# A hybrid layer: second norm's squares with the out-projection, its gain on up's weights, three groups' first products ahead, w_down's sums paced

## The chip, the cores and the metric

One core of a Trainium2 chip. The metric is device time in microseconds of one launch, as the median of several runs. The core has five engines that run their own instruction queues in order: PE (matmuls), DVE and ACT (elementwise work), POOL, and SP, which issues nearly all transfers here. "fp32r" is the type in which the kernel gives its float32 operands to PE.

## The reference

One layer on 1040 positions (16 meta tokens and 1024 tokens), width 1024:

```python
hn = rms_norm(h, norm1_gain)
proj = einsum('bld,de->ble', hn, w_in)
mixed = concat([diff_attention(q, k, v, ...), conformer_conv(u, ...)])
h = h + einsum('ble,ed->bld', mixed, w_out)
hn = rms_norm(h, norm2_gain)
a = relu(einsum('bld,df->blf', hn, w_up))      # 1024 -> 4096
h = h + einsum('blf,fd->bld', a * a, w_down)   # 4096 -> 1024
return h[:, N_META:]
```

with rms_norm(x, g) = x * rsqrt(mean(x * x) + 1e-6) * g, all in float32.

## The kernel before

The 1024 tokens are eight tiles of 128. Every product is made of three matmuls (`three`, L331), since each operand is split into a rounded part (hi, a copy on ACT) and the rest (lo, a difference on DVE); `halves` (L813) makes such a pair. The up- and down-projections use a Strassen scheme: the matrices are cut in 2 x 2 blocks, so that seven products take the place of eight, at the price of sums of blocks on DVE.

The stages follow one another: first norm and input projection, convolution, attention in 32 units with the convolution's out-projection between them, the attention's out-projection (`attn_out`, L696: one half of 512 columns of one tile; it loads the convolution's part, adds the product, stores h2 to DRAM), second norm, up, down. Of the 16 halves of `attn_out` eight lie among the attention units, for tiles 7 to 4, and use one of the two PSUM banks of the tag "x"; the other eight are `late_out` (L988), for tiles 3 to 0, behind attention.

The second norm is `normed(t)` (L830): it loads a tile of h2 again from DRAM (tile 0 is kept on chip), squares it on ACT (L839), takes the inverse root in two POOL steps (L124, L125), multiplies by it and by the gain row `grow` on DVE (xn, L845), and transposes xn on PE into two PSUM banks. The gain row is made at the very start by eight small matmuls, two copies and two stores (L172 to L183). `norm_first` (tiles 7 to 4) makes the operands 11 and 21; `norm_second` (tiles 3 to 0) combines them with its own rows into t1 to t4 and 22 (L866).

Up works in 16 groups of 256 columns of w_up. `up_prep(g)` loads four cells of 128 x 512 (tag "wr", six buffers, 256 KB each), sums them and writes seven pairs (tag "wp", six buffers). A group's products are numbered: 1 and 2 need only the operands of `norm_first`, 6, 4, 7, 5 and 3 need those of `norm_second`. For NE = 2 groups `up_early` (L974) makes products 1 and 2 in the middle of the norms. Product 3 of a group (`up_last`, L953) is made in the next group, with the four sums that become down's operands; they go to DRAM (asp). `down_sums` (L941) loads 2 MB of w_down, forms four sums in place and stores them (wsp); it is called in every second group.

The order on each engine's queue is set by a scheduler at build time: it goes through the instructions by priority (program order, mostly), with a model of their times, and takes what it believes ready; a tile of a tag waits for a free buffer of this tag. On the chip each queue then runs in this fixed order.

## Time and profile before

| | |
|---|---|
| median of 3 runs | 1186.49 us (1185.21 to 1188.16) |
| the profiled execution | 1185.49 us, span 1183.7 us, mean granted clock 0.983 |
| PE busy | 1112.7 us, 94% of the span |
| DVE busy | 819.4 us, 69% |
| ACT busy | 561.8 us, 47% |
| POOL busy | 135.9 us, 11% |
| transfers | 189.67 MB, mean 160 GB/s |

The span runs from the first to the last instruction. A table of stretches gives each engine's busy time in a piece of the span; the granted clock is the share of TensorE's full speed, 1.00 for 2.4 GHz. In a time line the bracket behind a row tells how long the engine stood idle before it and what ended that.

### The profile page before, as it was taken

What the parts mean: (1) busy time and instruction counts of PE and PEld (TensorE: products, weight loads), DVE (VectorE), ACT (ScalarE), POOL (GpSimd) and SP (SyncE); (2) the same over time, 40 slices, a digit from 0 to 9 for tenths busy, and PEclk for the clock granted to TensorE, in tenths of its full rate; (3) what the DMA queues carried; (4) which work ended last, traced back from release to release, by engine and by line L of the source; (5) the groups of instructions that cost most, each with busy time, mean ns of one, the idle gap of its engine ahead of it and who ended that gap; (6) DMA issues with size and microseconds to landing.
All of it is one profiled execution on the core that took longest, in us unless ns stands there. A gap on an engine that the chain in (4) does not pass through costs nothing.

```text
span 1183.7 us, 15731 instructions
## 1 busy us (share of the span) xinstructions
PE 1112.7 (94%) x5712; PEld 935.9 (79%) x5712; DVE 819.4 (69%) x1366; ACT 561.8 (47%) x1230; POOL 135.9 (11%) x145
## 2 busy tenths in 40 slices
PE   3999999999999999785999999999989999999998
PEld 2899888777788888674778877788868888888887
DVE  5669989967788788679678868866647544445430
ACT  6522155607767677546345545555636332333320
POOL 3100274414002252111000000000000000000000
PEclk9999999999999999898899999999999999999999
DMA  7302011000123321572699999844369765556610
GB/s 279 108 1 73 1 37 37 5 24 27 37 71 107 105 93 53 177 231 92 229 322 324 325 340 310 293 149 135 127 233 402 267 241 215 208 199 227 215 56 36
DMA packets 103230, 189.67 MB, mean 160 GB/s; under 512 B 7904, under 2 KB 42976, under 8 KB 97520
## 3 DMA queue, kind: packets, MB, share of 16 engines
q1 hardware_dynamic: 103152, 188.66, 46.1%
q8 instruction: 45, 0.74, 0.3%
q14 instruction: 33, 0.27, 0.1%
HBM read 129.39 MB, written 59.24 MB: 159 GB/s over the span
## 4 chain that ended last, share of the span: by engine, by line
PE 65%; DVE 14%; DMA 9%; issue 5%; ACT 4%; POOL 2%; SPq 0%; DVEq 0%; POOLq 0%; ACTq 0%
PE py L335 5%; PE py L333 5%; PE py L334 5%; PE px L334 5%; PE px L335 5%; PE px L333 5%; DMA wr<-in_w_up 3%; PE pu L334 3%; PE pu L335 3%; PE pu L333 3%; PE pq L334 2%; PE pq L335 2%; PE pq L333 2%; DMA wdr<-in_w_down 2%; DVE wp L816 2%
## 5 line engine op out<-in xcount | busy, mean ns | idle before, releaser
L816 DVE TENSOR_TENSOR pair<-rv,pair 128x2048 fp32r<-128x2048 f32 x56 | 126.7, 2288 | 120.2 <-ACT pair L815 120.2
L815 ACT ACTIVATE pair<-rv 128x2048 fp32r<-128x2048 f32 x56 | 105.1, 1911 | 169.2 <-PE py L335 85.7
L333 PE MATMUL py<-pair 128*128 128x512 f32 x256 | 99.6, 389 | 0.0
L334 PE MATMUL py<-pair 128*128 128x512 f32 x256 | 99.6, 389 | 0.0
L335 PE MATMUL py<-pair 128*128 128x512 f32 x256 | 99.6, 389 | 0.0
L333 PE MATMUL px<-pair 128*128 128x512 f32 x192 | 74.7, 389 | 0.0
L334 PE MATMUL px<-pair 128*128 128x512 f32 x192 | 74.7, 389 | 0.0
L335 PE MATMUL px<-pair 128*128 128x512 f32 x192 | 74.7, 389 | 0.0
L333 PE MATMUL pu<-xT,w 128*128 128x260 f32 x256 | 73.1, 288 | 1.2 <-ACT xT L128 1.2
L334 PE MATMUL pu<-xT,w 128*128 128x260 f32 x256 | 73.6, 288 | 0.0
L335 PE MATMUL pu<-xT,w 128*128 128x260 f32 x256 | 73.2, 286 | 0.0
L935 ACT ACTIVATE a<-a 128x512 f32<-128x512 f32 x64 | 39.3, 629 | 61.5 <-DVE a L819 31.8
L333 PE MATMUL px<-hnt,wp 128*128 128x512 f32 x128 | 51.8, 404 | 13.1 <-ACT hnt L815 9.6
L124 POOL TENSOR_SCALAR ms<-ss 128x1 f32<-128x1 f32 (+3 forms) x34 | 37.3, 1097 | 203.5 <-ACT junk L391 137.6
L815 ACT ACTIVATE wp<-wr 128x512 fp32r<-128x512 f32 x64 | 39.7, 626 | 43.2 <-PE pw L335 22.5
L819 DVE TENSOR_TENSOR wdr<-wdr 128x1024 f32<-128x1024 f32 x32 | 39.0, 1220 | 29.0 <-DMA wdr<-in_w_down 14.8
L335 PEld LDWEIGHTS py<-pair 128*128 128x128 f32 x256 | 48.0, 188 | 10.0
L334 PEld LDWEIGHTS py<-pair 128*128 128x128 f32 x256 | 48.0, 188 | 10.0
L333 PEld LDWEIGHTS py<-pair 128*128 128x128 f32 x256 | 48.0, 188 | 9.9
L815 ACT ACTIVATE wp<-s 128x512 fp32r<-128x512 f32 x48 | 30.1, 628 | 52.1 <-PE px L335 30.7
L334 PE MATMUL px<-hnt,wp 128*128 128x512 f32 x128 | 51.4, 402 | 1.5 <-DVE hnt L816 1.5
L335 PE MATMUL px<-hnt,wp 128*128 128x512 f32 x128 | 51.4, 402 | 0.0
(296 smaller groups left out, 3204.3 us busy)
## 6 DMA issues: line engine op xcount, KB each, us to landing
rv<-as SPq DMA_DIRECT2D x28, 1024.0 KB, 6.2
wr<-in_w_up SPq DMA_DIRECT2D x68, 256.0 KB, 4.6
as<-a SPq DMA_DIRECT2D x64, 256.0 KB, 3.4
wdr<-in_w_down SPq DMA_DIRECT2D x8, 2048.0 KB, 9.7
ws<-wdr SPq DMA_DIRECT2D x32, 512.0 KB, 4.0
rv<-ws SPq DMA_DIRECT2D x16, 1024.0 KB, 4.8
as<-as SPq DMA_DIRECT2D x48, 256.0 KB, 3.6
rv<-in_w_down SPq DMA_DIRECT2D x12, 1024.0 KB, 6.0
```

Of the source, the lines that this page charges most:

```text
L124: RS.tensor_scalar(ms, ss, eps, None, ALU.add)
L333: T.matmul(ps, st[0], mv[0], start=first, stop=False, skip_group_check=more)
L334: T.matmul(ps, st[0], mv[1], start=False, stop=False, skip_group_check=more)
L335: T.matmul(ps, st[1], mv[0], start=False, stop=last, skip_group_check=more)
L815: S.activation(hi, src, AF.Copy)
L816: (eng or V).tensor_tensor(out=lo, in0=src, in1=hi.bitcast(F32), op=ALU.subtract)
L819: eng.tensor_tensor(out=out, in0=a, in1=b, op=ALU.subtract)
L935: S.activation(c, c, AF.Relu)
```

## The change

The squares of the second norm are taken by `attn_out` from its own sum, half by half, with the result of the squaring written over the product's PSUM bank; the inverse roots `rs2` follow there. All tiles of `late_out` stay on chip (four buffers of half a tile), and the first two halves are made ahead of the first norms. In `normed` xn is now one ACT copy with the scale `rs2`, without the gain; reloaded tiles use the buffers "wr". The gain is put on w_up's rows after their load, in place on ACT, four pieces a load (`wload`), so the gain row and its making go. "wr" has two buffers of 512 KB, "wp" has seven.

Products 1 and 2 are made ahead for three groups, after all norms in program order, both in one PSUM bank; their two results go to DRAM and come back when the group's turn comes. In the group loop `up_last` moves behind product 2, and product 5 ahead of 7. The eight `down_sums` are spread over groups 0 to 11, and each begins with a copy on DVE that reads a result of its group, ahead of its load.

```diff
--- before.py
+++ after.py
@@ -48,11 +48,12 @@
 QDI = 1
 WR = 2
 W1T = 5
-UT = 7
-WRB = 6
+UT = 8
+WRB = 2
 WSB = 3
-WPB = 6
-NE = 2
+WPB = 7
+NE = 3
+HKB = 4
 RVB = 4
 
 
@@ -167,20 +168,6 @@
         nc.sync.dma_start(xs[0][:, t, :], x[t * P:(t + 1) * P, :])
     gains = cp.tile([P, 2, 8], F32, tag="gains", name="gains")
     nc.sync.dma_start(gains, ngains)
-
-
-    growd = dr.tile([P, D], F32, tag="growd", name="growd")
-    ones = sp.tile([P, P], F32, tag="tmp", name="ones", bufs=4)
-    G.memset(ones, D ** 0.5)
-    for hf in range(2):
-        bank = tr_bank("gtr")
-        for q in range(4):
-            dg = sp.tile([P, P], F32, tag="tmp", name="dg", bufs=4)
-            V.tensor_scalar(dg, ident, gains[:, 1, 4 * hf + q:4 * hf + q + 1], None, ALU.mult)
-            T.matmul(bank[:, q, :], ones, dg, start=True, stop=True)
-        gr = sp.tile([P, 512], F32, tag="tmp", name="gr", bufs=4)
-        S.activation(gr, bank.rearrange("p a b -> p (a b)"), AF.Copy)
-        nc.sync.dma_start(growd[:, 512 * hf:512 * hf + 512], gr)
 
     xT = []
     for c in range(4):
@@ -692,18 +679,25 @@
 
     h2d = [dr.tile([P, D], F32, tag=f"h2d{t}", name=f"h2d{t}") for t in range(NT)]
     h2t = {}
+    ssq = cp.tile([P, NT, 2], F32, tag="ssq", name="ssq")
+    rs2 = cp.tile([P, NT], F32, tag="rs2", name="rs2")
 
     def attn_out(pool, t, nh, keep=None):
+
         if keep is None:
             hs = tmp([P, 512], F32, "hs")
         else:
-            if nh == 0:
-                h2t[t] = keep.tile([P, D], F32, tag="h2k", name="h2k", bufs=1)
-            hs = h2t[t][:, 512 * nh:512 * nh + 512]
+            hs = keep.tile([P, 512], F32, tag="h2k", name="h2k", bufs=HKB)
+            h2t.setdefault(t, []).append(hs)
         nc.sync.dma_start(hs, cvo[t, nh])
         ps = half_out(pool, ma, state[0, nh], t)
         V.tensor_tensor(out=hs, in0=hs, in1=ps, op=ALU.add)
         nc.sync.dma_start(h2d[t][:, 512 * nh:512 * nh + 512], hs)
+        S.activation(ps, hs, AF.Square, scale=D ** -0.5, accum_out=ssq[:, t, nh:nh + 1])
+        if nh:
+            ms = small([P, 8], "ms", 4)[:, :1]
+            G.tensor_scalar(ms, ssq[:, t, 0:1], ssq[:, t, 1:2], EPS, ALU.add, ALU.add)
+            G.tensor_tensor(out=rs2[:, t:t + 1], in0=ms, in1=mhalf[:, :1], op=ALU.pow)
 
     uqs, pend = [], []
     for t in range(NT):
@@ -822,8 +816,6 @@
         eng.tensor_tensor(out=out, in0=a, in1=b, op=ALU.add)
 
 
-    grow = up.tile([P, D], F32, tag="wp", name="grow", bufs=WPB)
-    nc.sync.dma_start(grow, growd)
     hn = {}
     hraw = slot([P, 2, 4, 512], F32, "hraw")
 
@@ -832,18 +824,13 @@
         if t in h2t:
             hv = h2t[t]
         else:
-            hv = up.tile([P, D], F32, tag="wp", name="h2t", bufs=WPB)
-            nc.sync.dma_start(hv, h2d[t])
-        ss = small([P, 1], "ss")
-        junk = sp.tile([P, D], BF16, tag="tmp", name="junk2", bufs=4)
-        S.activation(junk, hv, AF.Square, accum_out=ss)
-        rs = small([P, 1], "rs")
-        rsqrt_of(rs, ss, D * EPS)
+            h2 = up.tile([P, D], F32, tag="wr", name="h2t", bufs=WRB)
+            nc.sync.dma_start(h2, h2d[t])
+            hv = h2[:, :512], h2[:, 512:]
         banks = []
         for kf in range(2):
-            xn = tmp([P, 512], F32, "xn")
-            V.scalar_tensor_tensor(xn, hv[:, 512 * kf:512 * kf + 512], rs[:, 0:1],
-                                   grow[:, 512 * kf:512 * kf + 512], ALU.mult, ALU.mult)
+            xn = sp.tile([P, 512], F32, tag="raw", name="xn", bufs=4)
+            S.activation(xn, hv[kf], AF.Copy, scale=rs2[:, t:t + 1])
             bank = pcm.tile([P, 4, P], F32, tag="mm", name="htr")
             for q in range(4):
                 T.transpose(bank[:, q, :], xn[:, q * P:(q + 1) * P], ident)
@@ -869,25 +856,26 @@
                 operand(name)
         r11, r21 = [hraw[:, j, :, col(t):col(t) + P] for j in range(2)]
         b12, b22 = normed(t)
-        r12, t1, t2, t4 = [cell(n) for n in ("r12", "t1", "t2", "t4")]
-        S.activation(r12, b12, AF.Copy)
+        t1, t2, t3, t4 = [cell(n) for n in ("t1", "t2", "t3", "t4")]
         sub(V, t1, b12, r11)
         sub(V, t2, b22, t1)
         halves(*parts("t2", t), t2)
         sub(V, t4, t2, r21)
         halves(*parts("t4", t), t4)
-        sub(V, r12, b22, r12)
-        halves(*parts("t3", t), r12)
+        sub(V, t3, t2, r11)
+        halves(*parts("t3", t), t3)
         halves(*parts("t1", t), t1)
         halves(*parts("22", t), b22)
 
 
     wu = {}
 
-    def wcell(g, j, c):
-        r = cell("wr", "wr", WRB)
-        nc.sync.dma_start(r, w_up[512 * j:512 * j + 512, 256 * g + P * c:256 * g + P * c + P].rearrange(
-            "(k p) f -> p k f", p=P))
+    def wload(g, j, n):
+
+        r = up.tile([P, 4, n], F32, tag="wr", name="wr", bufs=WRB, padded_shape=[P, 4, 256])
+        nc.sync.dma_start(r, w_up[512 * j:512 * j + 512, 256 * g:256 * g + n].rearrange("(k p) f -> p k f", p=P))
+        for k in range(4):
+            S.activation(r[:, k, :], r[:, k, :], AF.Copy, scale=gains[:, 1, 4 * j + k:4 * j + k + 1])
         return r
 
     def wpair(g, n, v):
@@ -896,11 +884,12 @@
         halves(*wu[g, n], v)
 
     def prep_early(g):
-        wpair(g, 1, wcell(g, 0, 0))
-        wpair(g, 2, wcell(g, 1, 0))
+        wpair(g, 1, wload(g, 0, P))
+        wpair(g, 2, wload(g, 1, P))
 
     def up_prep(g):
-        l11, l12, l21, l22 = [wcell(g, j, c) for c in range(2) for j in range(2)]
+        l1, l2 = [wload(g, j, 256) for j in range(2)]
+        l11, l21, l12, l22 = l1[:, :, :P], l1[:, :, P:], l2[:, :, :P], l2[:, :, P:]
         if g >= NE:
             wpair(g, 1, l11)
             wpair(g, 2, l12)
@@ -909,9 +898,9 @@
         sub(V, s2, s1, l11)
         wpair(g, 6, s2)
         wpair(g, 4, l22)
+        wpair(g, 5, s1)
         sub(V, l21, l11, l21)
         wpair(g, 7, l21)
-        wpair(g, 5, s1)
         sub(V, s4, l12, s2)
         wpair(g, 3, s4)
 
@@ -938,9 +927,10 @@
     asp = {(n, b): dr.tile([P, 4, 512], F32, tag=f"as{n}{b}", name=f"as{n}{b}") for b in range(4) for n in range(1, 8)}
     wsp = {(n, b): dr.tile([P, 4, 512], F32, tag=f"ws{n}{b}", name=f"ws{n}{b}") for b in range(4) for n in range(4, 8)}
 
-    def down_sums(g):
+    def down_sums(g, after):
 
         r = slot([P, 2, 2, D], F32, "wdr")
+        V.tensor_copy(r[:, 0, 0, 0:1], after[:, 0:1])
         nc.sync.dma_start(r, w_down[256 * g:256 * g + 512, :].rearrange("(q j p) n -> p q j n", j=2, p=P))
         r11, r12, r21, r22 = [r[:, :, j, 512 * k:512 * k + 512] for j in range(2) for k in range(2)]
         sub(V, r11, r12, r11)
@@ -964,66 +954,68 @@
         sub(V, a21, a11, a21)
         sub(V, s4, a12, s2)
         for n, v in ((1, a11), (2, a12), (4, a22), (5, s1), (6, s2), (7, a21), (3, s4)):
-            nc.sync.dma_start(asp[n, g // 4][:, g % 4, :], v)
-
-    def erow(name):
-        return up.tile([P, 512], F32, tag="e", name=name, bufs=2 * NE)
-
-    early = {}
+            if n > 1 or g >= NE:
+                nc.sync.dma_start(asp[n, g // 4][:, g % 4, :], v)
+
+    es = [dr.tile([P, 512], F32, tag=f"es{g}", name=f"es{g}") for g in range(NE)]
 
     def up_early(g):
+
         px = bank("px")
         up_product(g, 1, px, True)
-        s1 = erow("s1")
+        s1 = row("s1")
         S.activation(s1, px, AF.Copy)
-        py = bank("py")
-        up_product(g, 2, py, True)
-        a11 = erow("a11")
-        add(V, a11, s1, py)
-        relu2(a11)
-        early[g] = s1, a11
+        nc.sync.dma_start(es[g], s1)
+        up_product(g, 2, px, False)
+        a11 = row("a11")
+        S.activation(a11, px, AF.Relu)
+        S.activation(a11, a11, AF.Square)
+        nc.sync.dma_start(asp[1, g // 4][:, g % 4, :], a11)
 
     late = [(7 - k // 2, k % 2) for k in range(len(AOUT), 16)]
 
     def late_out(n):
         for _ in range(n):
             tn = late.pop(0)
-            attn_out(pcm, *tn, keep=None if tn[0] else up)
-
+            attn_out(pcm, *tn, keep=up)
+
+    late_out(2)
     for t in (7, 6):
         norm_first(t)
     late_out(2)
     for t in (5, 4):
         norm_first(t)
+    for g in range(NE):
+        prep_early(g)
     late_out(2)
-    prep_early(0)
     norm_second(3)
-    late_out(2)
-    up_early(0)
-    prep_early(1)
     norm_second(2)
     late_out(2)
-    up_early(1)
+    up_prep(0)
     norm_second(1)
-    up_prep(0)
     norm_second(0)
-
+    for g in range(NE):
+        up_early(g)
+
+    sums_at = {(8 * k) // 5: 2 * k for k in range(8)}
     held = None
     for g in range(NG):
-        if g in early:
-            s1, a11 = early.pop(g)
+        if g < NE:
+            s1, a11 = row("s1"), row("a11")
+            nc.sync.dma_start(s1, es[g])
+            nc.sync.dma_start(a11, asp[1, g // 4][:, g % 4, :])
         else:
             px = bank("px")
             up_product(g, 1, px, True)
             s1 = snap(px)
-        if held:
-            up_last(held)
-        if g >= NE:
             py = bank("py")
             up_product(g, 2, py, True)
             a11 = row("a11")
             add(V, a11, s1, py)
             relu2(a11)
+        if held:
+            up_last(held)
+        if g >= NE:
             up_product(g, 6, px, False)
             s2 = snap(px)
         else:
@@ -1035,23 +1027,22 @@
             up_prep(g + 1)
         pz = bank("pz")
         up_product(g, 4, pz, True)
+        pw = bank("pw")
+        up_product(g, 5, pw, True)
         up_product(g, 7, px, False)
         if g >= NE:
             s3 = snap(px)
         else:
             s3 = s1
             add(V, s3, s1, px)
-        a12 = row("a12")
+        a12, a22 = row("a12"), row("a22")
+        add(V, a22, s3, pw)
         sub(V, a12, s3, pz)
         relu2(a12)
-        pw = bank("pw")
-        up_product(g, 5, pw, True)
-        a22 = row("a22")
-        add(V, a22, s3, pw)
         relu2(a22)
         held = g, s2, pw, (a11, a12, a22)
-        if g % 2 == 0:
-            down_sums(g)
+        if g in sums_at:
+            down_sums(sums_at[g], s2)
     up_last(held)
     up_pool.__exit__(None, None, None)
     ps_c.__exit__(None, None, None)
```

## Rows read from the trace of the kernel before

**Rows 1.** Table of stretches: time, busy us per engine, clock, DMA share, GB/s.
```profile
431.00:491.60 60.60, 59.96 (x412) 52.03 (x410) 50.94 (x152) 43.65 (x143) 15.65 (x20) 1.00 0.19 62
491.60:571.00 79.40, 52.46 (x229) 42.29 (x229) 59.77 (x99) 41.26 (x79) 10.12 (x18) 0.81 0.60 193
571.00:760.00 189.00, 185.67 (x805) 151.39 (x804) 146.08 (x210) 88.75 (x161) 0.00 (x0) 0.99 0.93 314
760.00:863.00 103.00, 103.00 (x454) 85.02 (x454) 65.64 (x99) 57.99 (x98) 0.00 (x0) 1.00 0.47 156
863.00:885.00 22.00, 17.10 (x69) 13.43 (x69) 11.98 (x15) 8.60 (x13) 0.00 (x0) 0.92 0.53 185
```

**Rows 2.** Time line of PE, passage: start, length, line, idle before and releaser.
```profile
495.88 1.11 PE L654 MATMUL otr<-ident,osb 128*128 128x128 f32 x4 [4.24 <-DVE osb L651]
...
510.32 1.03 PE L849 MATMUL htr<-ident,xn 128*128 128x128 f32 x8
...
515.55 1.84 PE L849 MATMUL htr<-ident,xn 128*128 128x128 f32 x8 [4.20 <-DVE xn L845]
...
563.04 0.80 PE L333 MATMUL px<-hnt,wp 128*128 128x512 f32 x1 [9.61 <-ACT hnt L815]
```

**Rows 3.** Waits of PE, 570 to 885 us: total, times, longest.
```profile
PE pw L333 <- DVE a L822: 4.3, 3, 2.0
PE px L333 <- ACT sn L931: 3.5, 3, 2.9
```

**Rows 4.** Groups by shape, 491.6 to 571 us: busy, mean ns; idle before.
```profile
L845 DVE SCALAR_TENSOR_TENSOR xn<-h2t,rs,grow 128x512 f32<-128x512 f32 x14 | 9.9, 748 | 9.1 <-POOL rs L125 9.1
...
L839 ACT ACTIVATE junk<-h2t 128x1024 bf16<-128x1024 f32 x7 | 7.4, 1060 | 4.9 <-DMA h2t<-h2d 4.9
...
L839 ACT ACTIVATION_READ_ACCUMULATOR junk<-h2t 128x1 f32 x7 | 1.4, 197 | 0.0
...
L873 ACT ACTIVATE r<-htr 128x512 f32<-128x512 f32 x4 | 2.3, 587 | 3.6 <-PE htr L849 3.6
...
L816 DVE TENSOR_TENSOR wp<-wr,wp 128x512 fp32r<-128x512 f32 x6 | 3.9, 682 | 0.0
...
L822 DVE TENSOR_TENSOR sn<-s,px 128x512 f32<-128x512 f32 x1 | 0.7, 687 | 3.4 <-PE px L335 3.4
```

**Rows 5.** Groups by shape, ACT, whole span.
```profile
L815 ACT ACTIVATE wp<-wr 128x512 fp32r<-128x512 f32 x64 | 39.7, 626 | 43.2 <-PE pw L335 22.5 <-PE px L335 12.3 <-PE pz L335 5.2
...
L138 ACT ACTIVATE w<-raw,gains 128x512 fp32r<-128x512 f32 x40 | 26.8, 717 | 14.3 <-DMA raw<-in_w_in 9.6 <-PE pu L335 3.9 <-PE pq L335 0.8
...
L524 ACT ACTIVATE qt<-qs 128x256 fp32r<-128x256 f32 x24 | 10.0, 420 | 10.2 <-DVE qs L400 7.6 <-POOL wo L129 2.5
...
L128 ACT ACTIVATE u<-atr 128x128 fp32r<-128x128 f32 x8 | 2.2, 281 | 3.6 <-PE atr L621 3.6
...
L935 ACT ACTIVATE a<-a 128x512 f32<-128x512 f32 x64 | 39.3, 629 | 61.5 <-DVE a L819 31.8 <-DVE a L822 26.6 <-DMA as<-as 2.5
```

**Rows 6.** Waits, 491 to 571 us, and one row of SP's time line there.
```profile
POOL ms L124 <- ACT junk L839: 39.8, 6, 12.0
...
DVE xn L845 <- POOL rs L125: 9.1, 6, 3.7
...
528.39 0.32 SPq L836 DMA_DIRECT2D h2t<-h2d  x1
```

**Rows 7.** DMA issues, 491 to 571 us: count, KB each, median us to landing.
```profile
wr<-in_w_up SPq DMA_DIRECT2D x16, 256.0 KB, 5.6
...
h2t<-h2d SPq DMA_DIRECT2D x7, 512.0 KB, 5.8
```

**Rows 8.** Time line of ACT, 7 to 15 us.
```profile
10.09 0.71 ACT L138 ACTIVATE w<-raw,gains 128x512 fp32r<-128x512 f32 x1
13.10 0.60 ACT L182 ACTIVATE gr<-gtr 128x512 f32<-128x512 f32 x1 [2.29 <-PE gtr L180]
13.59 1.04 ACT L196 ACTIVATE junk<-mraw 16x1024 bf16<-16x1024 f32 x1
```

## The prediction, made before the changed kernel was run

> **What bounds the kernel now.** I read first the table of stretches, because the shares of the whole span hide it: PE is 94% busy over the span, so only the stretches where it is not busy can give time back. From 431 us to 491.6 us PE works 59.96 of 60.60 us; from 571 to 863 us it stands still for 3.3 us in all; but from 491.6 to 571.0 us, the passage from attention to the up-projection, it works 52.46 of 79.40 us at a mean granted clock of 0.81, and from 863 to 885 us 17.10 of 22.00 us [rows 1]. So the place to look is the passage. Its time line of PE shows six waits of 1.5 to 9.6 us; the first (4.24), the third (4.20) and the longest (9.61) stand in [rows 2]. They end on DVE (osb, xn) or on what DVE feeds (the ACT copy of an operand). DVE is the busiest elementwise engine there with 59.77 of 79.40 us, ACT has 41.26 [rows 1].
>
> Then the work itself. A matmul of 512 columns costs 0.2269 us at full rate (454 in 103.00 us, [rows 1]); a transpose 0.129 us (8 in 1.03 us, [rows 2]). The passage holds 96 matmuls of the last eight out-projection halves (21.8), 64 transposes (8.2), 4 more of the last attention unit (0.6) and 64 matmuls of up (14.5): 45.1 us. The wall is 79.4, so 26.9 us are idle and 7.4 us are work at the lower of the two clock levels (1.2 instead of 2.4 GHz): 8 transposes take 1.84 us after a wait instead of 1.03 [rows 2].
>
> Why it waits: per tile the chain is reload of h2 from DRAM, square on ACT, two POOL steps, xn on DVE. POOL waits 39.8 us for the squares, once 12.0 us, and DVE 9.1 us for POOL; the reload of tile 3 is issued only at 528.39 us [rows 6], after its two halves were stored.
>
> **Part by part, removed.** (a) growd: eight matmuls' worth of set-up. At the start ACT, in order, is done with its fourth weight row at 10.80, then copies gr at 13.10 after a wait of 2.29 us, and begins the squares at 13.59 [rows 8]. Without it the squares begin at most 2.8 us earlier. What follows also needs input transfers, so the gain is between 0 and 2.8 us; I take 2.3, since the ACT chain is what I see stand still.
> (b) In the passage DVE loses 16 xn at 0.748 = 12.0 us; ACT loses 8 squares at 1.060 + 0.197 and 4 copies r at 0.587, together 12.4 us [rows 4]. The POOL steps leave the chain, and tiles 3 to 1 no longer go through DRAM.
>
> **Added.** On ACT: 16 xn with a scale column at 0.717 (11.5 us); 8 squares of a half, 0.6 + 0.2 each (6.4); six early loads of four pieces 128x128 at 0.281 to 0.42, I take 0.281 + 0.09 for the column (0.717 less 0.626), 24 x 0.37 = 8.9; the first full group's eight pieces 128x256 at 0.420 + 0.09, 8 x 0.51 = 4.1; and the third early group's two copies, one snap and two steps of relu squared, 3.1 [rows 4, 5]. ACT goes from 41.3 to 41.3 - 12.4 + 34.0 = 62.9 us, DVE from 59.8 to about 48. **ACT takes over as the longest elementwise engine.** The cover for the new ACT work is PE's own work in the passage, 21.8 + 8.2 + 0.6 + 72 x 0.2269 (16.3, three early groups) = 46.9 us; it does not cover 62.9.
>
> **The sum for the passage.** The first pair of out-projection halves now comes before the norms and fills the first two waits. ACT can begin on the new work at about 496 us: the first half ends at 491.6 + 12 x 0.2269 = 494.3, its pair at 497.0, and a reload issued at 492 lands about there too. Of its 62.9 us about 10 (relu squared of the early groups, the last copies for later products) come after the first full product. DVE, the longest engine before, had 19.6 us idle, 9.1 of them for POOL [rows 6] and 3.4 at the end, when its sums were done and it waited for a product (sn, [rows 4]); without these it would have been busy 59.8 of 66.9 us, 0.89. With the same share ACT reaches the first full product at 496 + 53 / 0.89 = 555. At that point 46.9 us of PE work are done; before, 45.1 were done at 571.0, so 46.9 at 572.8. Gain **17.8 us**. Ends: ACT never idle, 496 + 53 = 549, 23.8 us; no sooner than the 563.04 of now [rows 2], 9.8 us.
>
> **Moved or slower.** (c) The squares of the eight halves inside attention (431 to 491.6 us) hold the out-projection's PSUM bank, one of two of that tag, for another 0.8 us each, where PE has 0.6 us of slack in the stretch and ACT 17 us [rows 1]: between 0 and 6.4 us lost; I take 1.5, because the two banks alternate and PE has other queued work. Two small POOL steps a tile lie beside a POOL that is busy 15.65 of 60.60 us.
> (d) The raw weights now have two buffers of 512 KB, one group, where there were six of 256 KB, one and a half. The four h2 reloads (two at a time), six early loads and the first group's two go through these in six rounds. A transfer lands after 5.6 us (256 KB) or 5.8 us (512 KB) [rows 7]; a round of the early loads adds 1.5 us of scaling, 0.63 of copy and 0.68 of difference [rows 4, 5], 8.4 us; two rounds of h2 take 7.2 each. That is 492 + 14.4 + 25.2 + 5.8 + 4.1 + about 3 for the sums and the first pair = 544, inside the 555, with 11 us to spare for queueing.
> After it the same two buffers make a loop: load (5.8), eight pieces of scaling (4.1), then sums and four pairs until the buffer is free. The pairs cost 4 x 0.63 on ACT and one last 0.68 on DVE, the sums 1.4: 14.5 us if nothing comes between. The first three groups have five products left, 60 x 0.2269 = 13.6 us. So PE waits about 1 us in each, and once more for the first loads; I take 4 us, between 0 and 16 (rival 1). Groups of seven products last 19.1 us and cover the loop. SP holds behind a load that waits for its buffer the stores of the products and the next loads; the one DVE copy that paces w_down's sums now waits for its buffer on DVE, where before only a load on SP waited for it; but the sums come every 1.6 groups, 30 us, so the buffer has long been stored, and I cost it at nothing. If it were late, the sums and differences of the running group would stand behind it on DVE, and PE behind those.
> (e) At the end, 2.9 of the 4.9 us idle [rows 1, 3] are the product that waits for a snapshot. The new order puts two products between, so this goes; the other wait, for a22, loses the product that covered its snapshot. Between -2 and +4.3 (the slow matmuls too); I take 2.5. For the middle of up I take 0: its 3.3 us of idle may go with the pacing (DMA was at 0.93 of its share from 571 to 760 us, [rows 1]), or come back by ACT's 4.1 us a group.
>
> Sum: 2.3 - 1.5 + 17.8 - 4 + 2.5 = 17.1 us. The profiled execution took 1185.49 us (span 1183.7), 1.0 under the median of 1186.49; so 1168.4 in its terms, **1169.4** against the median.
>
> **Rivals.** 1 (the other side, slower): the two-buffer loop becomes the bound of all of up. ACT runs in order; if all its other work of a group (two snapshots and six steps of relu squared, about 5, and two more copies, 1.3) falls inside the loop, it takes 14.5 + 6.3 = 20.8 us with a load of 5.8, and 22.8 with one of 7.8. From 19.1 on, PE pays the difference in each of 13 groups: 22 us at 20.8, 48 us at 22.8, and the first three groups cost 16 instead of 4: 1169.4 + 12 + 22 = 1203, up to 1229. For it: wr loads of 256 KB took up to 5.6 in the middle here with DMA at 0.60, and the first half of up is at 0.93 [rows 1, 7]. Against it: pairs are made almost a group ahead, and the transfers are paced. Chance 0.11.
> 2: ACT in DVE's place, with DVE's full inefficiency, 59.77 / 79.40 = 0.75: first full product at 496 + 53 / 0.75 = 567, gain 6 instead of 17.8: 1181. For it: ACT copies feed DVE differences and back, as the 9.61 us wait shows [rows 2]. Chance 0.19.
> The Trainium skill, page "ScalarE: Activation LUTs", section "Rules for kernel authors", says to use VectorE and not ScalarE for multiplications, which is against moving xn and the gain to ACT. In this passage the rows leave DVE with 48 us and ACT with 63, so by that rule rival 2 is what this split invites; no run here has shown the other split yet.
> 3: better than forecast: ACT hardly idle, no wait in the first groups: 6.0 and 4 more, 1159; with the small terms at their good ends (0.5, 1.5, 1.8) and the middle's 3.3 us, 1152. Chance 0.14.
> 4: it does little: the scheduler sets reloads and early loads behind each other on SP, the passage is as long as now and only start and end gain: 1184 to 1187. Chance 0.06.
>
> **How the numbers follow.** Forecast 0.50, 1161 to 1176; rivals 0.19, 0.14, 0.11, 0.06. The range 1152 to 1184 takes in the forecast, rival 2 and rival 3, and leaves out rivals 1 and 4, 0.17. A measurement of this kernel tells about 0.3%, 3.6 us, from no change: faster is below 1182.9 (0.50 + 0.14 + most of rival 2, 0.17 = 0.81), same to 1190 (0.07), slower beyond (0.12).
>
> **What would show it.** After: the stretch from the last attention matmul to the first full product about 64 us and not 74; ACT busier than DVE there; POOL with no wait in that chain; PE waits at groups 0 to 2 that end on ACT wp or on a wr load, of 1 to 3 us; start of the pu matmuls some 2 us earlier; PE still full from 431 to 491 us. Wrong would be: PE waits on wr loads through all of up (rival 1), DVE still the last to finish, or a start that did not move because input transfers set it.

## The result, and the profile after

The changed kernel takes 1158.82 us (median of 4 runs, 1157.35 to 1160.11); the kernel before, run beside it, 1187.33 (4 runs). The ratio is 0.976, 95% interval 0.9738 to 0.9782: 28.5 us faster. The profiled execution took 1157.35 us, its span is 1155.5 against 1183.7.

The table of stretches (columns as in [rows 1]), cut at the same places of the program: the last 60.6 us of attention, the passage up to the first full product, the first three groups of up, the middle of up, and the 22 us around its end.

```profile
413.10:473.70 60.60, 54.47 (x355) 45.56 (x356) 44.48 (x129) 41.51 (x140) 11.78 (x20) 1.00 0.16 53
473.70:535.00 61.30, 49.28 (x230) 39.90 (x230) 43.71 (x74) 52.92 (x121) 7.32 (x14) 0.92 0.50 159
535.00:575.00 40.00, 35.80 (x148) 28.34 (x148) 21.75 (x34) 22.70 (x48) 0.00 (x0) 0.96 0.72 244
575.00:760.00 185.00, 179.53 (x788) 147.21 (x787) 144.88 (x220) 122.57 (x244) 0.00 (x0) 1.00 0.83 290
834.00:856.00 22.00, 16.86 (x66) 13.24 (x66) 10.90 (x13) 7.04 (x10) 0.00 (x0) 0.92 0.52 185
```

Attention now ends at 473.7, not 491.4. In its last 60.6 us PE has 6.1 us of idle where it had 0.6 [rows 1]. In the passage ACT, 52.92 of 61.30 us, is the busiest elementwise engine, where DVE was (59.77 of 79.40). The first three groups lose 4.2 us of PE; the end, 16.86 of 22 us, is as it was.

Waits of PE from 473.7 to 860 us (total, times, longest), for [rows 3] and the waits of [rows 2]:

```profile
PE htr L836 <- ACT xn L833: 10.8, 5, 7.1
PE pw L320 <- ACT sn L920: 5.5, 4, 1.7
PE px L320 <- ACT wp L809: 3.8, 1, 3.8
PE px L320 <- ACT sn L920: 3.7, 1, 3.7
PE pw L320 <- DVE a L816: 1.4, 1, 1.4
```

Groups of ACT by shape in the passage (busy us, mean ns, idle before), for [rows 4]: the pieces of w_up with their gain, and xn.

```profile
L878 ACT ACTIVATE wr<-wr,gains 128x128 f32<-128x128 f32 x24 | 7.9, 432 | 1.0 <-DMA wr<-in_w_up 1.0
L878 ACT ACTIVATE wr<-wr,gains 128x256 f32<-128x256 f32 x8 | 3.4, 498 | 1.6 <-DMA wr<-in_w_up 1.6
L833 ACT ACTIVATE xn<-h2t,rs 128x512 f32<-128x512 f32 x8 | 5.4, 753 | 0.6 <-DMA h2t<-h2d 0.5
```

xn no longer waits for POOL's inverse root (9.1 us in [rows 4]). The largest surprise is at the other end of the program. The first rows of ACT's time line, and the first row of PE with the input projection (pu), for [rows 8]:

```profile
2.81 1.05 ACT L183 ACTIVATE junk<-mraw 16x1024 bf16<-16x1024 f32 x1 [0.60 <-DMA mraw<-in_meta]
5.16 1.06 ACT L183 ACTIVATE junk<-xs 128x1024 bf16<-128x1024 f32 x1 [1.19 <-DMA xs<-in_x]
```

```profile
16.25 0.72 PE L320 MATMUL pu<-xT,w 128*128 128x260 f32 x4
```

The first norm's squares began at 13.59 before [rows 8] and begin at 2.81 now; before, the first matmul of pu was at

```profile
33.32 1.23 PE L333 MATMUL pu<-xT,w 128*128 128x260 f32 x4 [1.22 <-ACT xT L128]
```

So the start moved by 17.1 us, not by 2.3. The pu matmuls end at 112.6 instead of 134.0.

### The profile page after: what moved, and what is told of

Read it like the earlier page. It is cut to its first block, busy times and chain, and to the rows that moved or that the text cites. A ratio compares the mean times of both kernels' runs of the same rounds, so it can differ in the third digit from the quotient of the medians.

```text
span 1155.5 us, 15787 instructions
## 1 busy us (share of the span) xinstructions
PE 1104.1 (96%) x5696; PEld 927.1 (80%) x5696; DVE 807.2 (70%) x1349; ACT 624.0 (54%) x1406; POOL 130.7 (11%) x144
## 4 chain that ended last, share of the span: by engine, by line
PE 67%; DMA 11%; DVE 10%; ACT 8%; issue 3%; POOL 1%; SPq 0%; ACTq 0%; DVEq 0%; POOLq 0%
DMA wr<-in_w_up 8%; PE py L322 5%; PE py L321 5%; PE py L320 5%; PE px L320 5%; PE px L321 5%; PE px L322 5%; PE pu L322 3%; PE pu L321 3%; PE pu L320 3%; PE pq L321 3%; PE pq L320 3%; PE pq L322 3%; DVE wp L810 2%; ACT wr L878 2%
## 5 line engine op out<-in xcount | busy, mean ns | idle before, releaser
L878 ACT ACTIVATE wr<-wr,gains 128x256 f32<-128x256 f32 (+1 forms) x152 | 62.7, 487 | 61.2 <-DMA wr<-in_w_up 61.1
L321 PE MATMUL pu<-xT,w 128*128 128x260 f32 x256 | 72.0, 284 | 0.0
L322 PE MATMUL pu<-xT,w 128*128 128x260 f32 x256 | 71.3, 283 | 0.0
L320 PE MATMUL pu<-xT,w 128*128 128x260 f32 x256 | 70.9, 282 | 0.0
L322 PE MATMUL pq<-w,xT 128*128 128x512 f32 x128 | 50.9, 398 | 0.0
L320 PE MATMUL pq<-w,xT 128*128 128x512 f32 x128 | 50.9, 397 | 0.0
L321 PE MATMUL pq<-w,xT 128*128 128x512 f32 x128 | 50.8, 397 | 0.0
L321 PEld LDWEIGHTS pu<-xT,w 128*128 128x128 f32 x256 | 47.9, 188 | 0.0
```

Of the source, the lines that this page charges most:

```text
L320: T.matmul(ps, st[0], mv[0], start=first, stop=False, skip_group_check=more)
L321: T.matmul(ps, st[0], mv[1], start=False, stop=False, skip_group_check=more)
L322: T.matmul(ps, st[1], mv[0], start=False, stop=last, skip_group_check=more)
L878: S.activation(r[:, k, :], r[:, k, :], AF.Copy, scale=gains[:, 1, 4 * j + k:4 * j + k + 1])
```

## The experiments

To see where each kernel stands, I read from its trace when PE began its last matmul of three steps (the u part of the input projection, the v part, attention; headed "ends") and its first matmul of down. The columns "attention" and "passage and up" are the differences between them. Times are of the profiled executions; the medians of all runs stand in the last column. The runs were taken in several groups, each with the kernel before beside it; its median there lay between 1186.95 and 1188.14, so differences of a microsecond or two between medians of different groups mean nothing.

| kernel | pu ends | v ends | attention ends | first product of down | attention | passage and up | median |
|---|---|---|---|---|---|---|---|
| before | 134.0 | 304.3 | 491.4 | 875.2 | 187.1 | 383.8 | 1187.33 |
| after | 112.6 | 277.0 | 473.7 | 846.8 | 196.7 | 373.1 | 1158.82 |
| setup_late | 130.4 | 295.7 | 487.8 | 873.2 | 192.1 | 385.4 | 1182.38 |
| setup_own_buffers | 121.2 | 291.7 | 483.9 | 869.7 | 192.2 | 385.8 | 1178.81 |
| setup_before_keys | 112.2 | 299.3 | 490.0 | 873.5 | 190.7 | 383.5 | 1187.19 |
| setup_back | 132.7 | 304.3 | 501.0 | 872.7 | 196.7 | 371.7 | 1182.79 |
| before_no_setup | 113.2 | 277.6 | 464.9 | 847.5 | 187.3 | 382.6 | 1160.08 |
| squares_in_norm | 113.3 | 277.7 | 465.1 | 858.1 | 187.4 | 393.0 | 1168.60 |
| squares_to_sbuf | 113.3 | 277.7 | 471.8 | 856.5 | 194.1 | 384.7 | 1165.77 |
| no_gain_on_up | 112.8 | 277.1 | 474.1 | 837.7 | 197.0 | 363.6 | 1148.95 |
| three_raw_buffers | 113.2 | 277.7 | 474.6 | 849.1 | 196.9 | 374.5 | 1157.56 |
| xn_on_dve | 112.9 | 277.2 | 473.7 | 838.6 | 196.5 | 364.9 | 1150.41 |
| gain_on_pool | 112.8 | 277.1 | 472.9 | 847.3 | 195.8 | 374.4 | 1157.83 |
| dve_xn_pool_gain | 113.5 | 277.9 | 473.0 | 859.2 | 195.1 | 386.2 | 1172.51 |

**Why the start moved.** The set-up of the gain row (`growd`, `ones`, `dg`, `gr`) has its tiles in the tag "tmp", as have the outputs `junk` of the first norm's squares. The theory: a tile waits for a buffer of its tag, so the scheduler puts the squares behind the set-up on ACT's queue. The rival: the start moved for another reason of the new order, and the set-up costs the 2.3 us of the prediction. The first three runs move the set-up in the kernel before (behind the input tiles, into buffers of its own, behind the convolution's projection), the fourth puts it back into the changed kernel, unused.

```diff
 setup_late, setup_before_keys: kernel before
-    growd = ...; ones = ...; for hf in range(2): ...      (L172 to L183)
+    the same block ahead of cvec / ahead of kst
 setup_own_buffers: kernel before
-    ones = sp.tile([P, P], F32, tag="tmp", name="ones", bufs=4)
+    ones = cvp.tile([P, P], F32, tag="gones", name="ones", bufs=1)
     (dg: tag "gdg", 2 buffers; gr: tag "ggr", 1 buffer)
 setup_back: kernel after
+    growd = ...; ones = ...; for hf in range(2): ...
```

> The kernel before with one edit: the gain row's set-up is written behind the eight tiles of the first norm, the rest is as before. Theory A (the set-up's tiles take the four buffers of the tag tmp, which the squares of the first norm need, so the squares stand behind it): the first pu matmul at about 16 us instead of 33, and 18 to 26 us less in all, near 1163. Theory B (only the set-up's own work on ACT, DVE and PE counts, 2 to 3 us, and the other 18 us at the start came with other parts of the change): 1184 or so. Theory C (the time won at the start is lost again inside the convolution and attention): pu early, total within 6 us of before.

> The kernel before with the set-up in its place, but its tiles in buffers of their own. Theory A: the squares start as early as with the set-up moved, the set-up's own copies stay on ACT, so pu starts 2 to 4 us later than there: about 1166. Theory B: no change, 1187. If the order of the queues and not the buffers counts: 1180 to 1187.

> The changed kernel with the gain row's set-up put back at its old place (its result is stored and read by nobody). Theory A: the first pu matmul back at about 33 us, and 18 to 26 us more than the changed kernel, 1177 to 1185. Theory B: 2 to 3 us more, 1161.

> The kernel before with the gain row's set-up written behind the convolution's projection, where its four buffers of the tag tmp stand in the way of neither the first norm nor the small tables. Nothing else is changed. If the start of the changed kernel is owed to those buffers alone: the last pu matmul at 112 to 115 us as in the changed kernel (134 before), the lead at the end of attention 15 to 22 us, and 1165 to 1172 in all. If the lead is given back in attention because DVE's deferred convolution work still has to be done: pu early, but 1178 to 1184.

Ratios: setup_late 0.9954 (0.994 to 0.9967), setup_own_buffers 0.9912 (0.9883 to 0.9942), setup_before_keys 0.999 (0.9973 to 1.0008), setup_back 0.9951 (0.9932 to 0.997). ACT's time lines of setup_back and of setup_own_buffers:

```profile
13.57 1.04 ACT L196 ACTIVATE junk<-mraw 16x1024 bf16<-16x1024 f32 x1
```

```profile
2.87 1.05 ACT L196 ACTIVATE junk<-mraw 16x1024 bf16<-16x1024 f32 x1 [0.65 <-DMA mraw<-in_meta]
```

With the set-up back in its place the changed kernel starts as late as before (13.57), and 24 of its 28.5 us are gone: 1182.79, as theory A said. With buffers of its own the set-up stands at the same line and the squares begin at 2.87. So the shared tag is what held the squares; this is shown. But the totals of the other three runs missed what that theory said for them: 1182.38 for 1163 (theory C's total), 1178.81 for 1166, 1187.19 for 1165 to 1172. With buffers of its own the set-up still costs 18.7 us (against the run without it, below). 8.0 of them are there at the end of pu, where PE, in order, stands at its matmuls; the other 10.7 come later, and I have not followed them. Where the set-up is moved, the next users of its tag come late. Waits of PE in setup_own_buffers:

```profile
PE gtr L180 <- DVE dg L179: 8.0, 3, 7.0
PE xtr L204 <- DVE xT L129: 4.0, 2, 3.5
```

in setup_late, where pu starts early (16.05) and ends late (130.4), with the row of ACT's time line that PE waits for:

```profile
PE pu L333 <- ACT th L355: 8.2, 1, 8.2
```

```profile
53.33 0.67 ACT L355 ACTIVATE th<-pu 128x260 f32<-128x260 f32 x2 [7.05 <-DVE ktab L259]
```

The table ktab is made from gk, the gain of the keys, which is loaded into a buffer of the tag "tmp". The load in setup_late, and in the run without the set-up (below):

```profile
45.99 0.43 SPq L248 DMA_DIRECT2D gk<-in_k_gain  x1
```

```profile
17.00 0.33 SPq L234 DMA_DIRECT2D gk<-in_k_gain  x1
```

And in setup_before_keys, PE from 110 to 300 us, and the first step of the keys on DVE (pm, also of the tag "tmp"), there and without the set-up:

```profile
PE ktr L431 <- DVE kt L129: 9.5, 4, 4.1
```

```profile
139.50 0.67 DVE L365 TENSOR_TENSOR pm<-pm,pq 16x512 f32<-16x512 f32 x1
```

```profile
117.85 0.67 DVE L364 TENSOR_TENSOR pm<-pm,pq 16x512 f32<-16x512 f32 x1
```

In setup_before_keys the lead of 21.8 us is whole at the end of pu (112.2) and lost by the end of v (299.3, 5.0 left). The keys' product begins at 112.4 there and at 113.3 without the set-up, but pm comes 21.7 us later. SP stands up to 48.0 us for the store of gr, but that is not it: the two stores are out at 126.6 and 138.6, and the next load comes at 144.2 even without the set-up; here it comes at 168.8, after 30.1 us of waiting for DVE's steps of the keys. That the tag holds gk and pm as it holds the squares is read from these rows and from the code; no run tests it by itself. Why attention is 191 to 192 us long in setup_late, setup_own_buffers and setup_before_keys, 4 to 5 more than before, isn't settled.

So I took the set-up out of the kernel before altogether.

```diff
-    growd = ...; ones = ...; for hf in range(2): ...
-    nc.sync.dma_start(grow, growd)
+    nc.sync.dma_start(grow, x[0:P, :])
```

> The kernel before with the set-up of the gain row taken out altogether; the row is loaded from the first rows of the input instead, so the same instructions multiply by wrong numbers. Theory 1 (the set-up's share of the start is all that the start gains, and the rest of the kernel keeps it): the pu matmuls end at 112 to 114 us as in the changed kernel, attention ends at 464 to 472, and the time is 1187 less 17 to 23, 1164 to 1170; then all other parts of the change together are worth 5 to 11 us. Theory 2 (an early start runs into convolution taps that are not yet done, so that the input projection or attention gives it back, as with the set-up ahead of the keys, 1187): attention ends later than 480 and the time is 1178 to 1187.

Measured: 1160.08, ratio 0.977 (0.9749 to 0.9791), 26.9 us. Theory 1, and further than it said: everything else in the change is together worth 1.3 us, which can't be told from nothing (0.977 against 0.976). Attention is as long as before (187.3 and 187.1), passage and up too (382.6 and 383.8). Its table of stretches (end of attention, passage) and its PE waits show the passage of [rows 1, 2] unchanged:

```profile
292.00:467.00 175.00, 171.31 (x1157) 149.89 (x1156) 144.26 (x362) 122.17 (x337) 39.08 (x42) 1.00 0.26 83
467.00:545.00 78.00, 53.23 (x232) 43.44 (x233) 59.24 (x95) 40.28 (x74) 10.19 (x18) 0.80 0.60 194
```

```profile
PE htr L835 <- DVE xn L831: 11.2, 3, 4.2
PE px L319 <- ACT hnt L801: 9.6, 1, 9.6
```

**The squares.** One run takes the squares of tiles 7 to 4 in `normed` again, one lets them write to SBUF and not over the PSUM bank.

```diff
 squares_in_norm: kernel after
     (attn_out, after the store of hs)
+        if keep is None:
+            return
     (normed, reloaded tiles)
+            S.activation(junk, h2, AF.Square, scale=D ** -0.5, accum_out=ssq[:, t, 0:1])
+            (the two POOL steps for rs2 behind it)
 squares_to_sbuf: kernel after
-        S.activation(ps, hs, AF.Square, ...)
+        junk = sp.tile([P, 512], BF16, tag="tmp", name="junk4", bufs=4)
+        S.activation(junk, hs, AF.Square, ...)
```

> The changed kernel, but for tiles 7 to 4 the squares are taken in the norm from the reloaded tile (one ACT step and two POOL steps a tile), not in the out-projection. If the eight squares cost attention its extra time: the way from the last product with the values' weights (277 us) to the last attention product (473.7) shortens from 196.7 to about 192, the passage gains ACT work of 4 x 1.26 = 5 us, so the total is 1155 to 1162. If attention is longer only because it starts earlier relative to DVE's backlog: still 196, and the total 3 to 5 us worse, 1163.

> The changed kernel with the squares of the out-projection written to a small SBUF tile and not over the product's PSUM bank, so the bank is free after the addition on DVE; the squares stay on ACT. If the attention stage lost its 7 to 10 us because the bank is held: PE waits in 380 to 480 us go down from about 7 us to 2, and 5 to 8 us less in all, 1152. If it lost them because ACT has 6 us more to do there: no change, 1159.

squares_in_norm: 0.9826 (0.9802 to 0.9851), 9.8 us over the changed kernel. Attention gets back its 187.4, so the squares cost it 9.3; passage and up take 19.9 longer, where the forecast had 5, and both of its totals were missed. Waits of PE inside attention (293 to 474 us), first after, then squares_in_norm:

```profile
PE ops L621 <- ACT uq L520: 2.5, 4, 0.8
PE atr L608 <- DVE ma L645: 1.5, 2, 0.8
PE ops L621 <- DVE osb L625: 1.2, 2, 0.7
```

```profile
PE ops L621 <- DVE osb L625: 0.5, 1, 0.5
PE ops L621 <- ACT uq L520: 0.5, 1, 0.5
PE atr L608 <- DVE u L130: 0.4, 1, 0.4
```

The waits are many, of at most 0.8 us, and end on ACT and on DVE, not on the bank. All of them come to 7.3 us after and 1.4 in squares_in_norm, 5.9 of the 9.3; PE is also busy some 3 us longer after (187.2 against 184.0). squares_to_sbuf, 0.981 (0.978 to 0.9839), agrees: without the bank held, attention is only 2.6 us shorter. But its squares take a buffer of the tag "tmp", as the sums hs do, so 2.6 is no clean price of the bank. That the rest is ACT's queue, where the squares stand ahead of the next unit's steps, is argued from these releasers and not shown by itself. squares_to_sbuf is 7 us slower in all, outside both of its forecasts; its passage and up lose 11.6, and I have not followed why.

**Gain and buffers in up.** One run leaves the gain on w_up out (the second norm's gain is then missing from the computation), one gives "wr" a third buffer.

```diff
 no_gain_on_up: kernel after
-        for k in range(4):
-            S.activation(r[:, k, :], r[:, k, :], AF.Copy, scale=gains[...])
 three_raw_buffers: kernel after
-WRB = 2
+WRB = 3
```

> The changed kernel without the scaling of w_up's rows on ACT; the second norm's gain is left out of the computation. It prices the 152 ACT steps of 0.41 us on average, 62.7 us of ACT. If ACT binds the passage and the two-buffer loop binds the first groups: the waits of xn (10.8 us) and of the first group's pairs (4.2) shrink, 6 to 12 us less, 1147 to 1153. If the scaling lies beside other work: within 3 us of 1159.

> The changed kernel with three buffers of 512 KB for raw weights and reloaded tiles where it has two. If the loop of load, scaling and pairs over two buffers is what PE waits for in the first groups (3.8 + 0.4 us and the slow clock behind it) and what makes ACT wait 61 us for loads: 4 to 8 us less, 1151 to 1155. If ACT's own work sets the passage: within 2 us of 1159.

no_gain_on_up 0.9671 (0.9636 to 0.9705), 9.9 us below the changed kernel, in its first range; three_raw_buffers 0.9736 (0.9711 to 0.9761), 1.3 below it, in its second. But in no_gain_on_up the waits for xn, which that first theory had shrink, are as long as after (10.8); only those for the first pairs are gone. Its wait for xn and its middle of up, then passage and middle of up in three_raw_buffers:

```profile
PE htr L836 <- ACT xn L833: 10.3, 5, 7.7
```

```profile
575.00:760.00 185.00, 183.25 (x807) 151.09 (x807) 141.82 (x215) 96.88 (x176) 0.00 (x0) 1.00 0.86 299
```

```profile
473.00:535.00 62.00, 44.09 (x208) 35.59 (x207) 44.34 (x75) 53.37 (x124) 7.72 (x14) 0.86 0.51 162
575.00:760.00 185.00, 183.94 (x811) 151.68 (x810) 149.13 (x222) 123.93 (x246) 0.00 (x0) 1.00 0.86 304
```

A third buffer gives PE 4.4 us in the middle of up (183.94 against 179.53), but in the passage it takes them back (44.09 of 62, where the changed kernel has 49.79): with a buffer free, the early loads come sooner and their scaling stands on ACT ahead of xn. The waits of PE on xn there are 17.2 us, once 11.8. So the two buffers do cost the middle a little.

To compare passages I count, from the end of attention, until PE has 60 matmuls of up behind it: 61.4 us after, 57.4 in no_gain_on_up, 67.0 in three_raw_buffers.

**Which engine.** xn to DVE; the gain row made behind attention and multiplied in by POOL; and xn on DVE with w_up's gain on POOL.

```diff
 xn_on_dve: kernel after
-            S.activation(xn, hv[kf], AF.Copy, scale=rs2[:, t:t + 1])
+            V.tensor_scalar(xn, hv[kf], rs2[:, t:t + 1], None, ALU.mult)
 gain_on_pool: no_gain_on_up, and
+    (grow: eight matmuls of ones and dg in tag "mm", two ACT copies, kept in SBUF)
+            G.tensor_tensor(out=xn, in0=hv[kf], in1=grow[:, 512 * kf:512 * kf + 512], op=ALU.mult)
+            S.activation(xn, xn, AF.Copy, scale=rs2[:, t:t + 1])
 dve_xn_pool_gain: xn_on_dve, and
-            S.activation(r[:, k, :], r[:, k, :], AF.Copy, scale=gains[...])
+            G.tensor_scalar(r[:, k, :], r[:, k, :], gains[...], None, ALU.mult)
```

> The changed kernel with the 16 multiplications xn on DVE instead of ACT. Theory 1 (ACT, 53.6 of 62 us busy from 473 to 535, is what PE waits for there, and DVE, 43.9, has room): the passage gets 3 to 8 us shorter, 1151 to 1156. Theory 2 (the wait follows whichever engine xn stands on, because xn then queues behind differences on DVE): waits for xn of 10 us or more that end on DVE, and 1159 to 1168.

> The changed kernel without the scaling of w_up; the gain row is made by eight small matmuls behind attention and kept on chip, and a POOL multiplication by it goes ahead of each of the 16 ACT copies xn. The result is the full layer again. Theory 1 (ACT's scaling, 62.7 us in all, is what up loses its 9.5 us to, and POOL with 7.3 of 62 us busy has room for 16 steps of about 1.34): 1149 to 1154, PE waits on xn up by no more than 4 us. Theory 2 (the POOL step lies in the chain of every tile and the eight matmuls of the row at 0.42 lie on PE): the passage gives the gain back, 1157 to 1166.

> The changed kernel with xn on DVE and, besides, the gain put on w_up's pieces by POOL instead of ACT; the result is the full layer. Theory 1 (what the gain on w_up costs is ACT's time, 62.7 us, most of all the 13 of it in the passage): 1144 to 1149, ACT from 473 to 535 at 38 us or less where it is 45.0 with xn on DVE alone. Theory 2 (ACT has room once xn is on DVE, so a step of 0.4 to 0.8 us on POOL for each of the 152 pieces only lengthens the way from load to first pair): 1150 to 1160, waits of DVE and ACT for a piece of POOL of more than the 35.8 us that DVE waited for ACT's pieces.

xn_on_dve is the best full kernel: 1150.41, ratio 0.9694 (0.9672 to 0.9716), 8.4 us below the changed one and below the range of its theory 1. Its passage, its xn group there, and its waits of PE:

```profile
473.00:535.00 62.00, 49.76 (x240) 41.19 (x241) 51.24 (x93) 45.00 (x108) 8.38 (x14) 0.92 0.50 162
```

```profile
L833 DVE TENSOR_SCALAR xn<-h2t,rs 128x512 f32<-128x512 f32 x8 | 3.5, 483 | 3.8 <-DMA h2t<-h2d 3.8
```

```profile
PE htr L836 <- DVE xn L833: 11.4, 4, 8.8
PE px L320 <- ACT sn L920: 1.2, 3, 0.7
```

One xn takes 0.483 us on DVE and 0.753 on ACT. The wait for xn stays (11.4 against 10.8): that half of theory 2 was right, and its price wrong. The longest wait, for the xn of the last tile, is 7.1 us after, 7.7 without the gain and 8.8 here; what sets it is open. In the passage the 60 matmuls of up are done after 59.5 us, 1.9 sooner, where theory 1 said 3 to 8. Most of the gain is behind the passage. PE is busy 184.37 of 185 us from 575 to 760 us, and the waits of pw and px for ACT's snapshots (5.5 and 3.7 after) shrink to 1.2. How ACT work done earlier in the passage frees those later waits I have not followed instruction by instruction.

gain_on_pool, 0.9751 (0.9734 to 0.9769), gives back 8.9 of the 9.9 us, as theory 2 said. Up is relieved of the scaling, but the passage loses it: its 60 matmuls of up are done after 68.5 us, where no_gain_on_up has 57.4. Rows of PE's and of ACT's time line at its head, and PE's waits for xn:

```profile
475.48 1.38 PE L827 MATMUL gtr<-dg,ones 128*128 128x128 f32 x10 [2.33 <-POOL ones L821]
```

```profile
476.68 0.60 ACT L828 ACTIVATE grow<-gtr 128x512 f32<-128x512 f32 x1 [2.46 <-PE gtr L827]
481.48 0.72 ACT L845 ACTIVATE xn<-xn,rs 128x512 f32<-128x512 f32 x1 [4.20 <-POOL xn L844]
```

```profile
PE htr L848 <- ACT xn L845: 12.6, 6, 6.2
```

The set-up again stands in front: its `ones` waits on POOL behind the last roots of attention, and PE and ACT wait for it, 2.33 and 2.46 us. The 4.20 us are POOL's own step: the multiplication by the gain (1.27 us) comes behind the reload of the tile. The clock granted in this passage is 0.83 (0.92 after). What each of these costs I have not separated.

dve_xn_pool_gain is 22.1 us slower than xn_on_dve: 1172.51, 0.9885 (0.9853 to 0.9917). A group of POOL over the whole span, PE's waits, and the middle of up:

```profile
L878 POOL TENSOR_SCALAR wr<-wr,gains 128x256 f32<-128x256 f32 x128 | 146.3, 1160 | 165.8 <-DMA wr<-in_w_up 124.6 <-DVE wdr L813 22.0 <-DVE a L816 19.2
```

```profile
PE px L320 <- ACT wp L809: 7.2, 6, 1.9
PE py L320 <- ACT wp L809: 2.8, 4, 1.2
```

```profile
575.00:760.00 185.00, 177.11 (x751) 140.19 (x750) 138.27 (x203) 85.91 (x156) 83.47 (x72) 0.99 0.80 277
```

A piece takes 1.160 us on average on POOL (0.918 at the least), where I had put 0.4 to 0.8, and 0.498 on ACT. The total lies outside both theories. Eight pieces are 9.3 us instead of 4.0, between a load and a pair, with two buffers: I read this as the loop of rival 1, made longer by 5.3 us, and PE now waits for first pairs (px, py for wp) in many groups. These waits are 10.0 of the 22.1 us; the rest I have not followed. ACT has more room than ever (85.91 of 185 us), so ACT's own time in the middle of up was not what cost there.

## Why the prediction was right, and where its steps were wrong

The time, 1158.8, lies in the range and on the right side, below the forecast's own 1161 to 1176 and in rival 3's numbers, though rival 3's reasons (ACT hardly idle, no wait in the first groups) did not hold: ACT was busy 0.86 of the passage, and the first groups lost 6.6 us. The terms of the sum came out otherwise, and two large errors partly cancelled, +25.0 in (a) and -8.1 in (c); that the time still fell in the range is in part luck. In profiled time, by the table above:

| term | predicted | measured | by |
|---|---|---|---|
| (a) start, to the end of v | +2.3 | +27.3 | before, after |
| (c) squares in attention | -1.5 | -9.6 | 196.7 against 187.1 |
| passage to the first full product | +17.8 | +17.9 | count of matmuls, below |
| (d) first three groups | -4 | -6.5 | below |
| middle of up and (e) end | +2.5 | -0.1 | below |
| sum to the first product of down | 17.1 | 28.4 | 875.2 less 846.8; the terms add to 29.0, 0.5 of it for four more transposes, counted in the passage |

**(a) is the step that failed.** "The squares begin at most 2.8 us earlier" took the instructions ahead of the squares on ACT's queue as work that has to come first. But only their place in the queue put them first. The input tiles had been there: after, the first squares wait for the transfer and start at 2.81, 10.8 us earlier. I had read how long ACT stood for gr (2.29 us, [rows 8]) and not why the squares stood behind gr at all; the shared tag was in the code. Of the 27.3 us, 10.8 are the squares' start; 6.3 more are gone by the first pu matmul (17.1), 4.3 more by its end (21.4), and 5.9 more by the end of v (27.3). Those later gains are seen in the milestones and I have not separated their causes. They are all the set-up's: before_no_setup has the same milestones within 0.6 us.

**(c)** had the sign and the wrong size, outside its bounds (0 to -6.4). I priced a held PSUM bank; writing elsewhere, in squares_to_sbuf, gave back 2.6 of it. What I left out, as far as the waits tell, is that eight halves put 6.4 us of ACT into a stretch where PE's small waits end on ACT, however idle ACT is on average: its 17 us of idle at the end of attention [rows 1] were no cover.

**The passage** came out at the size worked out, but not for the one reason given. At 535.0 PE has done 60 matmuls of up and stands where the kernel before stood at 571.0 with 64 (both with all 96 of the out-projection and all 64 transposes). With 4 x 0.2269 for the difference and 0.5 for four more transposes, 61.7 us after the end of attention against 79.6: 17.9. ACT took over from DVE as told, with 52.92 busy of 61.3 us, 0.86 against the 0.89 and 53 us assumed. Rival 2 (a share of 0.75) fell. But if ACT's time alone set the end, as the sum has it, taking 8.6 us of ACT out of the passage (from 473 to 535 us: 53.62 after, 45.02 in no_gain_on_up, 45.00 in xn_on_dve) would end it 9.7 us sooner; it ended 4.0 and 1.9 us sooner. So another limit stands at most 4 us behind ACT, which the sum does not have, and the agreement to 0.1 us is in part luck. The first full product came 61.4 us after the end of attention, for about 64; the kernel before had 71.6, not the 74 I wrote. POOL still waits for squares, but nothing in the chain waits for POOL.

**(d)** was mis-sized and partly mis-explained. From 535 to 575 us PE has done 147 matmuls, 33.4 us of work in 40 us: 6.6 lost (the kernel before did 176, 39.9, from 571 to 611 us), of which one wait of 3.79 on the ACT copy of a pair, at 561 us, has the predicted form. In the 40 us behind each kernel's own first full product PE does 148 matmuls after, 143 with a third buffer and 168 without the scaling. So the stretch loses its time to the scaling, and a third buffer does not give it back. Rival 1 did not come true here; dve_xn_pool_gain suggests that it stood close: with 5.3 us more of scaling a group the kernel lost 22.

**The middle and (e).** The middle lost 5.5 us of PE from 575 to 760 us, before 3.3 from 571 to 760; the waits on snapshots (pw for sn, 5.5 us) are new, and with the gain left out the stretch has 1.75. The DVE copies that pace w_down's sums waited 0.5 us in all, so costing them at nothing held. Against the work done, PE loses 13.8 us from 575 us to the first product of down, and 13.7 from 611 us before: no gain. At the end the wait for a snapshot that was to go is still there (3.7; 2.9 in [rows 3]), with pw's 1.4 beside it (2.0 before): PE 16.86 of 22 us against 17.10. "The new order puts two products between" took program order for queue order. On PE the last group's products run 1, 2, 4, 5, 6, 7, 3 in both kernels; the scheduler had 5 ahead of 6 already. Product 7 still waits for the snapshot of product 6, which stands on ACT behind a copy for down:

```profile
834.99 1.91 ACT L809 ACTIVATE pair<-rv 128x2048 fp32r<-128x2048 f32 x1 [1.24 <-DMA rv<-as]
837.33 0.57 ACT L920 ACTIVATE sn<-px 128x512 f32<-128x512 f32 x1
```

What each part is worth, from pairs of medians: the set-up gone, -26.9 (before to before_no_setup), or -24.0 from the other end (setup_back to after); the squares of tiles 7 to 4 in `attn_out`, -9.8 (squares_in_norm to after); the gain on w_up, +9.9 (no_gain_on_up to after). With the whole at -28.5, all the rest (the squares of the kept tiles, xn on ACT, the three early groups, the tiles kept, the new order and the paced sums) is left with -1.7 together. That is a difference of numbers that need not add up, and within what the medians can't tell; of these only xn was run alone.

The prediction weighed a rule of the Trainium skill, page "ScalarE: Activation LUTs", section "Rules for kernel authors", against moving xn to ACT: use VectorE for multiplications. The runs agree with the rule: 0.483 against 0.753 us for one, and 8.4 us for the kernel. It did not make rival 2 true; that the other savings of the passage outweighed it is my reading, not shown.

## What to carry to other kernels

A step "off the path" can still set it: look at which buffers it shares with what comes behind it, and ask of each instruction at the head of a queue whether its inputs had long been there. Cost a change by undoing each part, alone, from both ends: here one deletion at the start was worth as much as the whole, while two well-argued moves cancelled (-9.8 and +9.9). Before moving work to an idle engine, price it there by its own rows, and count it in every loop that a buffer closes. And read the order of the queues from the trace: the program's order is not it.

## What the runs showed of the hardware that was not expected

A multiplication of 128x256 float32 by a column takes 1.160 us on average on POOL, 0.918 at the least, and 0.498 on ACT; one of 128x512 takes 0.483 on DVE, where a difference of two such tiles takes 0.684 to 0.687. That DVE is faster with one tensor operand than with two agrees with the Trainium skill, page "VectorE: DVE Perf Modes", section "Mode 2×_2P — use both read ports for one tensor"; the POOL figure was measured beside a busy DVE, and I have no run of it alone.
